# One encoder step on a TensorE-bound core: remainders of ten weight tiles made by an adding DMA in place of eight native fp32 steps, and six sample products earlier

## The chip, the cores and the metric

The kernel runs on one core of a Trainium2 chip. TensorE (PE in the profile) multiplies; VectorE (DVE), ScalarE (ACT) and GpSimd (POOL) do the rest; transfers are issued from SyncE (SP) and from POOL. The metric is device time in microseconds of one execution: 2345.04 us before, the median of three runs from 2344.96 to 2345.13.

## The reference

A streaming encoder of two layers, for 256 prompt tokens and 8 x 16 sample tokens, 384 rows of 1024. Each layer is a mixer (a state-space one in layer 0, sliding-window attention in layer 1), and behind it a PEER layer, where the change lies. PEER is a mixture of 128 x 128 = 16384 experts of one row each:

```python
        cand = (v1[..., :, None] + v2[..., None, :]).reshape(PEER_TOKEN_BLOCK, PEER_HEADS, PEER_TOPK * PEER_TOPK)
        vs, ci = lax.top_k(cand, PEER_TOPK)
        eid = (e1 * PEER_NKEYS + e2).reshape(PEER_TOKEN_BLOCK, PEER_HEADS * PEER_TOPK)
        gate = jax.nn.softmax(vs.astype(jnp.float32), axis=-1).reshape(PEER_TOKEN_BLOCK, PEER_HEADS * PEER_TOPK)
        ue = jnp.take(u_tab, eid, axis=0)
        act = jax.nn.gelu(jnp.einsum('tkd,td->tk', ue, xb).astype(jnp.float32))
        ve = jnp.take(v_tab, eid, axis=0)
        return jnp.einsum('tk,tkd->td', (gate * act).astype(xb.dtype), ve)
```

Each token has a query for each of 8 heads; the best 16 of 128 first keys and of 128 second keys give 256 sums, the best 16 of which name the experts. So every token takes 128 rows of `u`, weighs gelu of its products with them by a softmax, and adds that many rows of `v`. All is float32.

## The kernel before

A PEER layer of this kernel has three stages. The **query phase** multiplies all 384 rows by the query weights in 16 tiles. **u** multiplies the prompt's 256 tokens with *all* 16384 rows of `u`, 128 rows a step, in 128 steps; each step leaves a 128 x 256 block in a big array `G` (two halves, `G[0]` and `G[1]`, 64 steps each). **V** multiplies `G`, once it is weighed by the gates, with all rows of `v`, again in 128 steps. The sample's 128 tokens don't use the dense products: POOL gathers each token's rows of `u` (128 gathers, one for each place k, into a ring of three tiles `gath`), and DVE multiplies and sums each with the tokens (`u_item`, a *sample product*). `tick(s)` sets when: the table `U_DUE` says how many of the 128 products must have been recorded by step s (0 to 63 is u's first half, 64 to 127 its second, 128 on V).

A float32 product is *split* on PE: ACT rounds a weight tile to `hi` (line 129), DVE makes the remainder `lo` = raw - hi (line 130), and `gemm_cols` (lines 165 to 167) adds hi x hi, hi x lo and lo x hi, 24 matmuls a step in u, and 12 by two in V (line 180). A *native* step multiplies float32 tiles as they are, with an exact copy `xf` of the tokens in u (lines 1212 and 1567) and `G` itself in V (line 1642), 8 instructions each without a remainder. Before, `NATIVE` names eight of u's steps and `NATIVE_V` twelve of V's. `hi` and `lo` go round in rings of two, to which two more are lent in the first half's first 56 steps (`more`); `raw` has four.

Beside u's first half runs the *routing*: Python generators, of which each `pull` records a piece. `sample` routes the sample's tokens, then `prompt` the 256 prompt tokens in two blocks. A piece is a top-16 (lines 1268 to 1272), the decoding of places (`decode`, one-hot products at 1323 and 1327, folds at 1331, sums `ES` at 1334) or the end (`route_end`: softmax, transposes on PE at 1363, copies at 1366, and for the sample the indices `eidU` at 1380). `route_end` yields `DELAY` times before its transposes, and for the sample a second time before its indices. In the loop over the first half's steps each step pulls two pieces of `sample` until it ends; only from then on does it pull one or two pieces of `prompt` and call `tick`. What `prompt` still holds after step 63 is recorded behind the loop. The second half needs all of it: `w_prep` builds from it one-hot tiles (`ob`, `og`, `oa`), `w_apply` multiplies them on PE (line 1609), `w_mult` puts the result on `G` (line 1615).

The order on each engine: in the query phase and u's first half a tile scheduler orders instructions by its own clock; in u's second half and in V they stand on PE, DVE, ACT and POOL as written. Buffers and semaphores follow from the rings.

Of the kernel before, what the change touches and what calls it, by code (L numbers as in the profile page):

```python
# [9 lines left out]
F32 = mybir.dt.float32  # L10
F32R = mybir.dt.float32r
# [4 lines left out]
AF = mybir.ActivationFunctionType  # L16
OP = mybir.AluOpType
AX = mybir.AxisListType

P = 128  # L20
D = 1024
KD = D // P
NB = 3
NP = 256
# [20 lines left out]
RG = 32 // GR  # L45
TURN = 8
GSCALE = 2.0 ** 15
NATIVE = range(4, 56, 7)
NATIVE_V = range(3, 63, 5)
TAIL = 2  # L50
DONE = (2, 0, 1)
GLAG = 2
DELAY = (4, 8)
EARLY = (4, 1)

GD = 2
# [1 line left out]
I_DUE = (206, 250)  # L58
PACE = 1.5
AHEAD = 2 * 64 - 5  # L60
U_DUE = ((64, 22), (128, 68), (192, 115), (206, P))
V_DUE = [82, 85, 90, 96, 103, 148, 156, 162, 167, 173, 178, 183, 188, 193, 199, 211,
         217, 222, 227, 232, 237, 243, 247, 252]
V_SLOTS = [(1, e, 66, 64 + e) for e in range(28, 60, 4)] + [(0, e, 128 + e + 5, 256) for e in (0, 4, 8, 12, 20, 24, 28, 32, 56, 60)] + [(0, 16, 209, 256)]
# [3 lines left out]
def encoder_step(ctx: ExitStack, tc: tile.TileContext, t_in, t_out):  # L68
    nc = tc.nc
    sync, act, dve, pool, pe = nc.sync, nc.scalar, nc.vector, nc.gpsimd, nc.tensor  # L70
    n_names = [0]

    def T(pl, shape, dt=F32, tag=None, bufs=None):
        n_names[0] += 1
        return pl.tile(shape, dt, tag=tag, name=f"{tag}_{n_names[0]}", **({} if bufs is None else {"bufs": bufs}))
# [41 lines left out]
    gcol = T(const, [P, 5, KD], F32, tag="gcol")  # L117
# [29 lines left out]
    def load_raw(src, n=D):  # L147
        raw = ring(n, F32, "raw", 4)
        sync.dma_start(raw, src)
        return raw  # L150

    def load_split(src, n=D):
        return split_raw(load_raw(src, n), n)
# [63 lines left out]
    def fill(pl):  # L217
        T(pl, [P, 56], F32, tag="fill")
# [909 lines left out]
    def peer(l):  # L1128
        with ExitStack() as c:
# [13 lines left out]
            G = [T(gpools[0], [P, HE, NP], F32, tag="G0"), None]  # L1143
# [32 lines left out]
            turned = {}  # L1176
# [27 lines left out]
            close_h()  # L1204
            xfctx = tc.tile_pool(name="pxf", bufs=1, side="right")
            xfpool = xfctx.__enter__()
            xf = T(xfpool, [P, KD, NP], F32, tag="xf")
            fill(xfpool)

            def exact(k):  # L1210

                act.activation(xf[:, k], turned[k][:, :NP], AF.Copy, scale=gcol[:, 2 + l, k:k + 1])

            def ready(k):
                return split(qhi[:, k], qlo[:, k], turned[k], scale=gcol[:, 2 + l, k:k + 1])

            with in_order():
                turn(range(6), [2])
                ahead = [bank([P, NT]) for _ in range(2)]
                hi1 = ring(D, F32R, "hi", 2)  # L1220
                lo1 = ring(D, F32R, "lo", 2)
                act.copy(hi1, raws[1])
                for k in range(KD):
                    ready(k)
                    if k in (1, 2):
                        exact(k - 1)
                    ks = slice(k * P, (k + 1) * P)
                    pe.matmul(ahead[0], wq[0][0][:, ks], qhi[:, k], start=(k == 0), stop=False)
                    pe.matmul(ahead[1], hi1[:, ks], qhi[:, k], start=(k == 0), stop=False)
                    pe.matmul(ahead[0], wq[0][0][:, ks], qlo[:, k], start=False, stop=False)  # L1230
                    pe.matmul(ahead[1], hi1[:, ks], qlo[:, k], start=False, stop=False)
                    pe.matmul(ahead[0], wq[0][1][:, ks], qhi[:, k], start=False, stop=(k == KD - 1))
                    if k in (1, 2):
                        turn([k + 5], range(NB))
                for k in range(2, KD):
                    exact(k)
                dve.tensor_tensor(lo1, raws[1], hi1.bitcast(F32), op=OP.subtract)
                for k in range(KD):
                    pe.matmul(ahead[1], lo1[:, k * P:(k + 1) * P], qhi[:, k], start=False, stop=(k == KD - 1))
                wq.append(load_split(t_in["p_w_q"][l, 2]))  # L1240
# [100 lines left out]
            def route_end(b):  # L1341
# [10 lines left out]
                if b == 2:  # L1352
                    dve.tensor_scalar(es[0], es[0], float(NKEY), float(l * NKEY * NKEY), op0=OP.mult, op1=OP.add)
                    dve.tensor_tensor(es[0], es[0], es[1], op=OP.add)
                for _ in range(DELAY[b == 2]):
                    yield
# [10 lines left out]
                if b == 2:  # L1367
                    lay = T(one, [P, GR + 1, P], F32, tag="gath", bufs=3)
                    for g_ in range(GR + 1):
                        dve.tensor_tensor(lay[:, g_].rearrange("p (q c r) -> p q c r", c=4, r=RG),  # L1370
                                          (group(ps[:, 1], g_) if g_ < GR else group(ps[:, 0], GD)).unsqueeze(1).to_broadcast([P, GR, 4, RG]),
                                          same_q.unsqueeze(2).unsqueeze(3).to_broadcast([P, GR, 4, RG]), op=OP.mult)
                    for _ in range(DELAY[1]):
                        yield
# [40 lines left out]
            for ct in range(2 * PH):  # L1415
                if ct < 2:
                    ps = ahead[ct]
                else:
                    ps = bank([P, NT])
# [136 lines left out]

            def u_weights(e2):

                if e2 in NATIVE:
                    return load_raw(t_in["u_t"][l, e2]), None  # L1560
                return load_split(t_in["u_t"][l, e2])

            def u_products(e2, wt):
                ps = bank([P, NP])
                if wt[1] is None:
                    for k in range(KD):
                        pe.matmul(ps, wt[0][:, k * P:(k + 1) * P], xf[:, k], start=(k == 0), stop=(k == KD - 1))  # L1567
                else:
                    gemm_cols(ps, wt, xs[0], xs[1], 0, NP)
                return ps  # L1570

            def u_gelu(e2, ps):
                act.activation(G[e2 // HE][:, e2 % HE], ps, AF.Gelu_apprx_tanh)
# [46 lines left out]
            def v_weights(e2):  # L1620

                if e2 in NATIVE_V:
                    return load_raw(vtab[e2]), None
                return load_split(vtab[e2])

            def v_acts(e2):

                if e2 in NATIVE_V:
                    return None
# [29 lines left out]
            start = [0]  # L1659

            def tick(s):

                room[0] = min(room[0] + PACE, PACE)
                s0, n0 = start[0], 0
                for s1, n1 in U_DUE:
                    if s < s1:
                        break
                    s0, n0 = s1, n1
                want = P if s >= U_DUE[-1][0] else n0 + (n1 - n0) * (s + 1 - s0) // (s1 - s0)
                while done["u"] < want:  # L1670
# [29 lines left out]

            busy = True
            xs = [qhi, qlo]
            for e2 in range(HE):
                j = e2 - (HE - TURN)
                if j == 0:
                    more.clear()
                    lent.__exit__(None, None, None)
                    xfctx.__exit__(None, None, None)
                    xpool = tc.tile_pool(name="px", bufs=1, side="right")
                    xp = xpool.__enter__()  # L1710
                    xhi = T(xp, [P, KD, NP], F32R, tag="xhi")
                    xlo = T(xp, [P, KD, NP], F32R, tag="xlo")
                    T(xp, [P, 8], F32, tag="gap")
                u_gelu(e2, u_products(e2, u_weights(e2)))
                if j >= 0:
                    ks = slice(2 * (j // 2), 2 * (j // 2) + 2)
                    x_, q_ = ((xhi, qhi), (xlo, qlo))[j % 2]
                    pin(act.copy(x_[:, ks], q_[:, ks, :NP]))
                if busy:
                    busy = pull(sample, 2)  # L1720
                    if not busy:
                        start[0] = e2 + 1
                        fetch_u(0)
                        fetch_u(1)
                else:
                    pull(prompt, 2 if e2 % 4 == 0 else 1)
                    tick(e2)
# [17 lines left out]
            wt = u_weights(HE)  # L1745
            held = in_order(HELD + (mybir.EngineType.Pool,))
            held.__enter__()
            for e2 in range(HE):
# [8 lines left out]
                wt = nxt  # L1757
# [19 lines left out]
            for e2 in range(2 * HE):  # L1777
                if mult:
                    w_mult(*mult.pop())
                while n < 2 * HE and n <= e2 + (2 if n < AHEAD else 1):  # L1780
                    if n == AHEAD:
                        more.clear()
                    wt = v_weights(n)
# [154 lines left out]
```

## Time and profile before

| | |
|---|---|
| median of three runs | 2345.04 us |
| the profiled execution's own time, its span | 2350.95 us, 2349.2 us |
| PE busy in the span | 2295.5 us (98%) |
| DVE, ACT, POOL busy | 1982.0 (84%), 1252.2 (53%), 764.2 us (33%) |
| layer 0: u's first half, second half, V | 453 to 649, 649 to 866, 866 to 1265 us |
| layer 1: u's first half, second half, V | 1514 to 1713, 1713 to 1926, 1926 to 2330 us |
| DMA share in u's first half, in V | 0.57 to 0.71, 0.99 |

A row of the timeline is start, duration, engine, line, operation and tiles, with the idle time before it and what ended that in brackets. Durations overlap a little: an instruction of DVE starts some 0.08 us before the one ahead of it is through, so what one costs is read from start to start.

### The profile page before, as it was taken

What the parts mean: (1) busy time and instruction counts of PE and PEld (TensorE: products, weight loads), DVE (VectorE), ACT (ScalarE), POOL (GpSimd) and SP (SyncE); (2) the same over time, 40 slices, a digit from 0 to 9 for tenths busy, and PEclk for the clock granted to TensorE, in tenths of its full rate; (3) what the DMA queues carried; (4) which work ended last, traced back from release to release, by engine and by line L of the source; (5) the groups of instructions that cost most, each with busy time, mean ns of one, the idle gap of its engine ahead of it and who ended that gap; (6) DMA issues with size and microseconds to landing.
All of it is one profiled execution on the core that took longest, in us unless ns stands there. A gap on an engine that the chain in (4) does not pass through costs nothing. (4 is left out here: it accounts for less than half of the span.)

```text
span 2349.2 us, 43880 instructions
## 1 busy us (share of the span) xinstructions
PE 2295.5 (98%) x16340; PEld 1957.4 (83%) x16341; DVE 1982.0 (84%) x4235; ACT 1252.2 (53%) x2393; POOL 764.2 (33%) x779
## 2 busy tenths in 40 slices
PE   7999999999999999999999999999999999999998
PEld 6899988999998997667776778999999997667775
DVE  5999956979988999888876676979998999888876
ACT  5665624344466676554444555334476666554443
POOL 1323300012245334545563100011145324545562
PEclk9999999999999999999999999999999999999999
DMA  5554444366799889999996515367799889999997
GB/s 200 188 194 174 160 152 162 130 220 243 252 349 340 302 309 325 385 370 398 409 419 259 164 64 179 120 208 250 238 355 339 315 306 331 384 367 394 413 419 280
DMA packets 178086, 649.72 MB, mean 277 GB/s; under 512 B 21248, under 2 KB 23152, under 8 KB 175472
## 3 DMA queue, kind: packets, MB, share of 16 engines
q1 hardware_dynamic: 100944, 365.85, 42.6%
q0 software_dynamic: 76928, 281.07, 32.0%
q8 instruction: 128, 2.10, 0.4%
q14 instruction: 86, 0.70, 0.1%
HBM read 630.62 MB, written 18.06 MB: 276 GB/s over the span
## 5 line engine op out<-in xcount | busy, mean ns | idle before, releaser
L129 ACT CAST hi<-raw 128x1024 fp32r<-128x1024 f32 (+1 forms) x426 | 444.2, 1043 | 607.1 <-PE bank L166 251.6
L130 DVE TENSOR_TENSOR lo<-raw,hi 128x1024 fp32r<-128x1024 f32 (+1 forms) x426 | 515.4, 1210 | 172.8 <-ACT hi L129 151.8
L1434 POOL DMA_INDIRECT gath<-in_p_u,eidU x226 | 292.2, 1293 | 830.6 <-DVE gath L1483 514.0
L167 PE MATMUL bank<-xhi,lo 128*128 128x256 f32 (+1 forms) x1088 | 307.4, 282 | 6.1 <-DVE lo L130 3.8
L165 PE MATMUL bank<-xhi,hi 128*128 128x256 f32 (+1 forms) x1088 | 311.6, 287 | 0.0
L166 PE MATMUL bank<-xlo,hi 128*128 128x256 f32 (+1 forms) x1088 | 305.3, 281 | 0.0
L1434 POOL DMA_INDIRECT G<-in_p_v,eidT x192 | 222.8, 1160 | 76.4 <-issue 53.6
L165 PE MATMUL bank<-qhi,hi 128*128 128x256 f32 (+1 forms) x784 | 232.3, 296 | 0.0
L167 PE MATMUL bank<-qhi,lo 128*128 128x256 f32 (+1 forms) x784 | 227.0, 290 | 2.2 <-DVE lo L130 2.2
L166 PE MATMUL bank<-qlo,hi 128*128 128x256 f32 (+1 forms) x784 | 228.1, 291 | 0.0
L167 PEld LDWEIGHTS bank<-xhi,lo 128*128 128x128 f32 x1088 | 204.4, 188 | 10.2 <-DVE lo L130 7.2
L1597 ACT ACTIVATE oa<-ioh,e2T 128x128 f16<-128x128 f16 x512 | 163.3, 390 | 92.2 <-PE bank L1609 71.4
L165 PEld LDWEIGHTS bank<-xhi,hi 128*128 128x128 f32 x1088 | 204.5, 188 | 9.5 <-issue 5.7
L180 PE MATMUL bank<-hi,phi 128*128 128x512 f32 x632 | 206.1, 405 | 1.5 <-ACT phi L129 1.5
L129 ACT CAST hix<-raw 128x1024 fp32r<-128x1024 f32 x118 | 123.9, 1050 | 156.7 <-PE bank L180 56.8
L166 PEld LDWEIGHTS bank<-xlo,hi 128*128 128x128 f32 x1088 | 204.5, 188 | 0.6 <-issue 0.2
L180 PE MATMUL bank<-lo,phi 128*128 128x512 f32 x632 | 197.7, 392 | 0.9 <-DVE lo L130 0.9
L180 PE MATMUL bank<-hi,plo 128*128 128x512 f32 x632 | 196.4, 390 | 0.0
L130 DVE TENSOR_TENSOR lox<-raw,hix 128x1024 fp32r<-128x1024 f32 x118 | 143.6, 1217 | 19.6 <-ACT hix L129 15.2
L180 PEld LDWEIGHTS bank<-hi,phi 128*128 128x128 f32 x632 | 113.6, 188 | 49.4 <-ACT phi L129 19.1
L167 PEld LDWEIGHTS bank<-qhi,lo 128*128 128x128 f32 x784 | 147.7, 188 | 2.6 <-DVE lo L130 2.6
L166 PEld LDWEIGHTS bank<-qlo,hi 128*128 128x128 f32 x784 | 148.5, 189 | 0.4
(416 smaller groups left out, 5518.5 us busy)
## 6 DMA issues: line engine op xcount, KB each, us to landing
raw<-in_u_t SPq DMA_DIRECT2D x256, 512.0 KB
raw<-in_p_v SPq DMA_DIRECT2D x256, 512.0 KB
raw<-in_w_in SPq DMA_DIRECT2D x32, 512.0 KB
raw<-in_p_w_q SPq DMA_DIRECT2D x32, 512.0 KB
raw<-in_w_z SPq DMA_DIRECT2D x16, 512.0 KB
s<-in_state_ssm SPq DMA_DIRECT2D x8, 1024.0 KB
out_sm_ssm<-s SPq DMA_DIRECT2D x8, 1024.0 KB
raw<-in_w_out SPq DMA_DIRECT2D x16, 512.0 KB
```

Of the source, the lines that this page charges most:

```text
L129: act.copy(hi, raw)
L130: dve.tensor_tensor(lo, raw, hi32, op=OP.subtract)
L165: pe.matmul(ps, whi[:, s], xhi[:, k, c0:c1], start=(k == 0), stop=False)
L166: pe.matmul(ps, whi[:, s], xlo[:, k, c0:c1], start=False, stop=False)
L167: pe.matmul(ps, wlo[:, s], xhi[:, k, c0:c1], start=False, stop=(k == KD - 1))
L180: mm = pe.matmul(halves[hf], x, w[:, hf * n:(hf + 1) * n], start=s_, stop=e_)
L1434: pool.indirect_dma_start(out=tile_, out_offset=None, in_=tab, in_offset=bass.IndirectOffsetOnAxis(ap=idx, axis=0))
L1597: act.activation(a[:, i], ioh, AF.Square, scale=-1.0, bias=e2T[:, t, 0:1])
```

## The change

In u's first half the eight native steps go. Instead, for the ten steps of `BY_DMA` (4, 9, ... 49), `u_ahead` loads the raw tile by SP into a place of `G[0]` that is written late (52 to 56 or 56 to 60, in turn); `u_summed` has ACT write `dhi`, the rounded tile, and `dlo`, the negated raw tile, and has POOL issue a DMA that adds the raw tile to `dlo`. The products of such a step are the same 24 matmuls, with the 16 on `dhi` first and the 8 on `dlo` last. It is called four steps ahead of its use; `dhi` and `dlo` have one tile each, where `xf` stood. In V, nine steps are native instead of twelve. `DELAY`'s second number, for the sample, goes from 8 to 12. `U_DUE` asks for 28 sample products by step 64 instead of 22, 72 by step 128 instead of 68, and as many as before from there on.

```diff
--- before.py
+++ after.py
@@ -45,12 +45,13 @@
 RG = 32 // GR
 TURN = 8
 GSCALE = 2.0 ** 15
-NATIVE = range(4, 56, 7)
-NATIVE_V = range(3, 63, 5)
+BY_DMA = range(4, 53, 5)
+BY_DMA_AHEAD = 4
+NATIVE_V = range(4, 63, 7)
 TAIL = 2
 DONE = (2, 0, 1)
 GLAG = 2
-DELAY = (4, 8)
+DELAY = (4, 12)
 EARLY = (4, 1)
 
 GD = 2
@@ -58,7 +59,7 @@
 I_DUE = (206, 250)
 PACE = 1.5
 AHEAD = 2 * 64 - 5
-U_DUE = ((64, 22), (128, 68), (192, 115), (206, P))
+U_DUE = ((48, 15), (64, 28), (128, 72), (192, 115), (206, P))
 V_DUE = [82, 85, 90, 96, 103, 148, 156, 162, 167, 173, 178, 183, 188, 193, 199, 211,
          217, 222, 227, 232, 237, 243, 247, 252]
 V_SLOTS = [(1, e, 66, 64 + e) for e in range(28, 60, 4)] + [(0, e, 128 + e + 5, 256) for e in (0, 4, 8, 12, 20, 24, 28, 32, 56, 60)] + [(0, 16, 209, 256)]
@@ -1204,13 +1205,7 @@
             close_h()
             xfctx = tc.tile_pool(name="pxf", bufs=1, side="right")
             xfpool = xfctx.__enter__()
-            xf = T(xfpool, [P, KD, NP], F32, tag="xf")
-            fill(xfpool)
-
-            def exact(k):
-
-                act.activation(xf[:, k], turned[k][:, :NP], AF.Copy, scale=gcol[:, 2 + l, k:k + 1])
-
+            summed = {}
             def ready(k):
                 return split(qhi[:, k], qlo[:, k], turned[k], scale=gcol[:, 2 + l, k:k + 1])
 
@@ -1222,8 +1217,6 @@
                 act.copy(hi1, raws[1])
                 for k in range(KD):
                     ready(k)
-                    if k in (1, 2):
-                        exact(k - 1)
                     ks = slice(k * P, (k + 1) * P)
                     pe.matmul(ahead[0], wq[0][0][:, ks], qhi[:, k], start=(k == 0), stop=False)
                     pe.matmul(ahead[1], hi1[:, ks], qhi[:, k], start=(k == 0), stop=False)
@@ -1232,8 +1225,6 @@
                     pe.matmul(ahead[0], wq[0][1][:, ks], qhi[:, k], start=False, stop=(k == KD - 1))
                     if k in (1, 2):
                         turn([k + 5], range(NB))
-                for k in range(2, KD):
-                    exact(k)
                 dve.tensor_tensor(lo1, raws[1], hi1.bitcast(F32), op=OP.subtract)
                 for k in range(KD):
                     pe.matmul(ahead[1], lo1[:, k * P:(k + 1) * P], qhi[:, k], start=False, stop=(k == KD - 1))
@@ -1556,15 +1547,37 @@
 
             def u_weights(e2):
 
-                if e2 in NATIVE:
-                    return load_raw(t_in["u_t"][l, e2]), None
-                return load_split(t_in["u_t"][l, e2])
+                return summed.pop(e2, None) or load_split(t_in["u_t"][l, e2])
+
+            raws_ = {}
+
+            def u_ahead(e2):
+
+                e = 52 + 4 * (BY_DMA.index(e2) % 2)
+                raws_[e2] = G[0][:, e:e + 4].rearrange("p e t -> p (e t)")
+                sync.dma_start(raws_[e2], t_in["u_t"][l, e2])
+
+            def u_summed(e2):
+
+                raw = raws_.pop(e2)
+                hi = T(xfpool, [P, D], F32R, tag="dhi")
+                lo = T(xfpool, [P, D], F32R, tag="dlo")
+                if e2 == BY_DMA[0]:
+                    fill(xfpool)
+                act.copy(hi, raw)
+                act.activation(lo, raw, AF.Copy, scale=-1.0)
+                pool.dma_start(lo.bitcast(F32), raw, accum_op=OP.add)
+                summed[e2] = hi, lo
 
             def u_products(e2, wt):
                 ps = bank([P, NP])
-                if wt[1] is None:
+                if e2 in BY_DMA:
+                    for x in xs:
+                        for k in range(KD):
+                            pe.matmul(ps, wt[0][:, k * P:(k + 1) * P], x[:, k, :NP],
+                                      start=(x is xs[0] and k == 0), stop=False)
                     for k in range(KD):
-                        pe.matmul(ps, wt[0][:, k * P:(k + 1) * P], xf[:, k], start=(k == 0), stop=(k == KD - 1))
+                        pe.matmul(ps, wt[1][:, k * P:(k + 1) * P], xs[0][:, k, :NP], start=False, stop=(k == KD - 1))
                 else:
                     gemm_cols(ps, wt, xs[0], xs[1], 0, NP)
                 return ps
@@ -1700,6 +1713,7 @@
 
             busy = True
             xs = [qhi, qlo]
+            u_ahead(BY_DMA[0])
             for e2 in range(HE):
                 j = e2 - (HE - TURN)
                 if j == 0:
@@ -1712,6 +1726,10 @@
                     xlo = T(xp, [P, KD, NP], F32R, tag="xlo")
                     T(xp, [P, 8], F32, tag="gap")
                 u_gelu(e2, u_products(e2, u_weights(e2)))
+                if e2 + BY_DMA_AHEAD in BY_DMA:
+                    u_summed(e2 + BY_DMA_AHEAD)
+                    if e2 + BY_DMA_AHEAD + 5 in BY_DMA:
+                        u_ahead(e2 + BY_DMA_AHEAD + 5)
                 if j >= 0:
                     ks = slice(2 * (j // 2), 2 * (j // 2) + 2)
                     x_, q_ = ((xhi, qhi), (xlo, qlo))[j % 2]
```

Lines below are those of the program they belong to; the changed one's are some 8 lower. The first place is DVE at the end of u's first half in layer 0. Before, from the second one-hot product of the last prompt piece on, through the remainders of steps 59, 60 and 61, to the first copies of the transposed sums:

```order
L1327 TENSOR_TENSOR oh_6882<-oh_6882,ixb_6880 128x2048
L130 TENSOR_TENSOR lo_7010<-raw_7007,hi_7009 128x1024
L1483 SCALAR_TENSOR_TENSOR gath_6845,au_5239<-gath_6845,xg_3874 128x1024
L1331 TENSOR_TENSOR oh_6882<-oh_6882 128x8x128
L130 TENSOR_TENSOR lo_7046<-raw_7043,hi_7045 128x1024
L1331 TENSOR_TENSOR oh_6882<-oh_6882 128x8x64
L1331 TENSOR_TENSOR oh_6882<-oh_6882 128x8x32
L1334 TENSOR_TENSOR ES_5927<-oh_6882 128x64 x2
L1483 SCALAR_TENSOR_TENSOR gath_6774,au_5239<-gath_6774,xg_3874 128x1024
L130 TENSOR_TENSOR lo_7087<-raw_7084,hi_7086 128x1024
L1366 COPY gcols_7076<-bank_7077 128x128
L1366 CAST e1T_3683<-bank_7077 128x256
```

And in the changed kernel, from the remainder of step 65 (`lo_7382`) on; the remainder of step 66 comes behind the copies that follow here:

```order
L131 TENSOR_TENSOR lo_7382<-raw_7379,hi_7381 128x1024
L1595 TENSOR_TENSOR ob_7410<-ioh_74,e1T_3683 128x512
L1314 TENSOR_TENSOR oh_7188<-ij_7150,io_637_3870 128x2048
L1474 SCALAR_TENSOR_TENSOR gath_7057,au_5405<-gath_7057,xg_3864 128x1024
L1598 TENSOR_TENSOR og_7412<-ob_7410,g_601_3685 128x1024
L1613 TENSOR_TENSOR oa_7420<-ioh_74,e2T_3684 128x512
L1318 TENSOR_TENSOR oh_7188<-oh_7188,ixb_7186 128x2048
L1474 SCALAR_TENSOR_TENSOR gath_7232,au_5405<-gath_7232,xg_3864 128x1024
L1322 TENSOR_TENSOR oh_7188<-oh_7188 128x8x128
L1474 SCALAR_TENSOR_TENSOR gath_7275,au_5405<-gath_7275,xg_3864 128x1024
L1322 TENSOR_TENSOR oh_7188<-oh_7188 128x8x64
L1322 TENSOR_TENSOR oh_7188<-oh_7188 128x8x32
L1325 TENSOR_TENSOR ES_6156<-oh_7188 128x64 x2
```

The one-hot products, folds and sums of the last prompt piece, which stood between the remainders of steps 58 to 61, now stand behind that of step 65, with the gate tiles of the second half and four sample products among them. The second place is PE, where step 60's last matmul and the transposes of the gates and sums into one bank stood before so:

```order
L167 MATMUL bank_7049<-qhi_3702,lo_7046 128x256
L1363 MATMUL bank_7077<-ident_69,gate_6967 128x128
L1363 MATMUL bank_7077<-ident_69,ES_5927 128x128
L165 MATMUL bank_7090<-qhi_3702,hi_7086 128x256
L1363 MATMUL bank_7077<-ident_69,ES_5927 128x128
L166 MATMUL bank_7090<-qlo_3703,hi_7086 128x256
L167 MATMUL bank_7090<-qhi_3702,lo_7087 128x256
L165 MATMUL bank_7090<-qhi_3702,hi_7086 128x256
```

And now, from the last matmuls of step 63, on `qhi` and `qlo`, to the first of step 64, on `xhi` and `xlo`:

```order
L167 MATMUL bank_7320<-qlo_3703,hi_7316 128x256
L168 MATMUL bank_7320<-qhi_3702,lo_7317 128x256
L1354 MATMUL bank_7351<-ident_69,gate_7268 128x128
L1354 MATMUL bank_7351<-ident_69,ES_6156 128x128 x2
L166 MATMUL bank_7385<-xhi_7005,hi_7375 128x256
L167 MATMUL bank_7385<-xlo_7006,hi_7375 128x256
L168 MATMUL bank_7385<-xhi_7005,lo_7376 128x256
```

The three transposes went from beside step 61 to the place between steps 63 and 64.

## The prediction

> **What bounds the kernel now.** I read the busy line of the page first, then the busy time by stretches of layer 0.
>
> ```profile
> PE 2295.5 (98%) x16340; PEld 1957.4 (83%) x16341; DVE 1982.0 (84%) x4235; ACT 1252.2 (53%) x2393; POOL 764.2 (33%) x779
> ...
> 452.80:505.00 52.20, 51.55 (x419) 50.52 (x418) 40.81 (x144) 24.04 (x36) 4.65 (x4) 1.00 0.57 192
> 505.00:580.00 75.00, 75.00 (x599) 73.34 (x598) 70.02 (x255) 32.14 (x49) 14.64 (x10) 1.00 0.70 245
> 580.00:649.00 69.00, 67.96 (x563) 66.93 (x563) 67.46 (x224) 34.32 (x54) 13.67 (x11) 1.00 0.71 249
> 649.00:700.00 51.00, 48.43 (x495) 46.71 (x495) 45.35 (x69) 36.72 (x78) 26.50 (x23) 1.00 0.95 358
> 700.00:866.00 166.00, 164.56 (x1671) 154.30 (x1670) 150.28 (x230) 110.56 (x225) 63.35 (x53) 1.00 0.88 315
> 920.00:1265.00 345.00, 345.00 (x1896) 247.75 (x1895) 287.93 (x433) 169.23 (x303) 185.64 (x153) 1.00 0.99 391
> ```
>
> The columns after the stretch are its length, then PE, weight loads, DVE, ACT and POOL busy, the granted clock, the DMA share and GB/s. TensorE sets the pace: in u's first half (452.8 to 649) it is busy 194.5 of 196.2 us, from 700 to 866 164.6 of 166, in V all of 345. But in the first half VectorE is nearly as full: from 505 to 649 it is idle 144 - 70.02 - 67.46 = 6.5 us. So an edit that lightens PE there can only gain if DVE comes along. ACT has half of its time free, and the DMA share of 0.57 to 0.71 stands against 0.99 in V.
>
> **The change on PE.** Each layer loses eight native products in u and three in V; the steps become split products of 24 and 12 matmuls.
>
> ```profile
> 464.38 3.61 PE L1567 MATMUL bank<-xf,raw 128*128 128x256 f32 x16
> 467.64 0.47 PE L165 MATMUL bank<-qhi,hi 128*128 128x256 f32 x1
> ...
> 470.56 0.28 PE L165 MATMUL bank<-qhi,hix 128*128 128x256 f32 x1
> ...
> 473.29 0.27 PE L1363 MATMUL bank<-ident,gate 128*128 128x128 f32 x1
> ```
> ```profile
> 883.91 0.70 PE L180 MATMUL bank<-hi,phi 128*128 128x512 f32 x2
> ...
> 886.76 3.59 PE L1642 MATMUL bank<-raw,G 128*128 128x512 f32 x8
> 890.19 0.63 PE L1609 MATMUL bank<-og,oa 128*128 128x64 f16 x16
> ```
>
> A native step and the split step behind it go from 464.38 to 470.56, 6.18 us; the next split step goes from 470.56 to 473.29, 2.73. So a native step is 3.45. A split step is 2.73 here, and at most (196.2 - 8 x 3.45) / 56 = 3.0 with all other matmuls of the stretch counted in; I take 2.80, near the lower end, since few other matmuls lie between, and 0.65 us saved for each: 8 x 0.65 = 5.2 us a layer. In V the native step is 890.19 - 886.76 = 3.43, the split one 886.76 - 883.91 = 2.85, 0.6 to 0.75 saved with its spread over other steps; 3 x 0.7 = 2.1 us a layer. Those three steps need three more remainders on DVE, while four sample products of the same length leave that stretch, so DVE is not worse there. PE alone would give -2 x (5.2 + 2.1) = -14.6 us.
>
> **The change on DVE.** Two remainders fewer in the first half (54 of 64 steps instead of 56), and six sample products more (28 instead of 22). And the order moves: the prompt's pieces are pulled only once the sample's are through, which `DELAY` puts eight pulls, four steps, later, so the end of the prompt's routing is recorded behind the loop. In the order its last part, with the sums `ES`, stands on DVE behind the remainder of step 65, and on PE its three transposes, which stood beside step 61, stand between steps 63 and 64. PE cannot begin step 64 before them. What that piece takes is read from the same instructions before:
>
> ```profile
> 631.98 1.22 DVE L1327 TENSOR_TENSOR oh<-oh,ixb 128x2048 bf16<-128x2048 bf16 x1
> 633.12 1.22 DVE L130 TENSOR_TENSOR lo<-raw,hi 128x1024 fp32r<-128x1024 f32 x1
> ...
> 635.39 0.69 DVE L1331 TENSOR_TENSOR oh<-oh 128x1024 bf16<-128x1024 bf16 x1
> 636.00 1.22 DVE L130 TENSOR_TENSOR lo<-raw,hi 128x1024 fp32r<-128x1024 f32 x1
> 637.13 0.74 DVE L1331 TENSOR_TENSOR oh<-oh 128x512 bf16<-128x512 bf16 x2
> 637.91 0.36 DVE L1334 TENSOR_TENSOR ES<-oh 128x64 f32<-128x64 bf16 x2
> 638.19 1.22 DVE L1483 SCALAR_TENSOR_TENSOR gath<-gath,xg 128x1024 f32<-128x1024 f32 x1
> 639.33 0.08 DVE L1483 DVE_READ_ACCUMULATOR gath<-gath,xg 128x1 f32 x1
> ...
> 647.16 1.23 DVE L130 TENSOR_TENSOR lo<-raw,hi 128x1024 fp32r<-128x1024 f32 x1
> 649.88 1.23 DVE L130 TENSOR_TENSOR lo<-raw,hi 128x1024 fp32r<-128x1024 f32 x1 [1.50 <-ACT hi L129]
> 651.03 0.41 DVE L1582 TENSOR_TENSOR ob<-ioh,e1T 128x512 f16<-128x512 f16 x1
> 651.48 0.69 DVE L1585 TENSOR_TENSOR og<-ob,g 128x1024 f16<-128x1024 f16 x1
> 652.09 0.42 DVE L1600 TENSOR_TENSOR oa<-ioh,e2T 128x512 f16<-128x512 f16 x1
> ```
>
> A row's start to the next row's start is what it holds DVE for: 1.15 us for a remainder, 1.14 for `oh<-oh,ixb` (the other one-hot product has the same shape) and for a sample product; 0.61 for the first fold of `oh`, 0.7 for the other two, 0.28 for `ES`, 0.45 for `ob`, 0.61 for `og`, 0.4 for `oa`. From the start of step 65's remainder to the end of `ES` the changed order has one remainder, `ob`, `og`, `oa`, two one-hot products, three folds, two sums and three sample products: 1.15 + 0.45 + 0.61 + 0.4 + 2 x 1.14 + 0.61 + 0.7 + 0.28 + 3 x 1.14 = 9.9 us. With 0.4 for the three transposes (the one at 473.29 above is busy 0.27, and such matmuls overlap), step 64 starts 10.3 us after the remainder of step 65.
>
> When does that remainder start? Before, the rows of step 63's last and step 64's first product, and of ACT's cast for step 65, are these:
>
> ```profile
> 648.60 0.28 PE L167 MATMUL bank<-qhi,lo 128*128 128x256 f32 x1
> 648.71 0.28 PE L165 MATMUL bank<-xhi,hi 128*128 128x256 f32 x1
> ...
> 648.79 1.05 ACT L129 CAST hi<-raw 128x1024 fp32r<-128x1024 f32 x1 [0.88 <-PE bank L166]
> ```
>
> The cast of step 65 waited for step 63's last use of the buffer, and its remainder followed at 649.88, 1.17 us after PE was through with step 63. This ring is as short after the change. If PE sets the pace, step 63 ends at 648.71 - 5.2 = 643.5, the remainder of step 65 starts at 644.7, and step 64 at 655.0: an idle PE for 11.5 us, and 6.3 us later than before. If DVE sets the pace: up to step 65's remainder it has two remainders fewer and two sample products more (24 of the 28), and 5.2 us of routing less (2 x 1.14 + 0.61 + 0.7 + 0.28, and 1.3 behind the transposes). Against that stands the later start of the samples: its indices come four steps later.
>
> ```profile
> 492.57 0.29 DVE L1380 CAST eidU<-bank 128x128 int32<-128x128 f32 x1 [3.75 <-PE bank L1378]
> 493.14 1.06 POOL L1434 DMA_INDIRECT gath<-in_p_u,eidU  x1 [97.39 <-DVE gU L1381]
> 498.56 1.22 DVE L1483 SCALAR_TENSOR_TENSOR gath<-gath,xg 128x1024 f32<-128x1024 f32 x1 [5.61 <-DMA gath<-in_p_u,eidU]
> ```
>
> Here DVE has nothing to do for 3.75 and 5.61 us, and four steps more of waiting (11.2 us) are filled with remainders and pieces of routing to about half, 6 us lost. That makes step 65's remainder 0.8 us later than 647.16 + 1.14 = 648.3, 649.1, and step 64 start at 659.4: 10.7 later than before. Of the 6.5 us that DVE had idle a part takes this up. Between 6.3 and 10.7 I take **7.7 us a layer**, nearer to the lower end, since PE is the fuller of the two.
>
> **What follows behind the stall.** In the second half the DVE waits of PE may be given back, since loads and casts run ahead while PE stands still.
>
> ```profile
> PE bank L167 <- DVE lo L130: 2.4, 4, 0.9
> PE bank L167 <- issue: 1.4, 2, 0.9
> PE bank L167 <- DVE lo L130: 1.2, 2, 0.8
> PE bank L167 <- issue: 0.4, 1, 0.4
> ```
>
> These are all waits of PE in u's second half (total, times, longest), the first two rows of layer 0, the last two of layer 1: 3.8 and 1.6 us, 2.7 on average. More than that cannot come back there, and nothing may. I take all of it, for two sample products (2.3 us of DVE) leave this stretch too.
>
> **The adding DMA.** Its chain for one step is a cast, a gelu and a negated copy on ACT (at most three times the 1.05 us of a cast, 3.2), the issue on POOL, and the landing; its low products need it 4 steps and 16 of 24 matmuls after the buffers come free, 4 x 2.8 + 1.9 = 13.1 us. With 1.1 for the issue the landing has 8.8 us. No such transfer is in this trace; the nearest row is the gather issued at 493.14, whose product starts at 498.56, 5.4 us later. At two steps (29 and 49) the adding DMA stands on POOL's queue behind a gather that waits for a sample product, which comes after the remainder of three steps earlier: 3 x 2.8 + 1.9 - 1.14 - 1.3 - 1.1 = 6.8 us are left. Between 5.4 and an unknown upper end I take 5.4: hidden, no cost. The rows of POOL's issues beside a busy DVE:
>
> ```profile
> 565.50 0.94 POOL L1434 DMA_INDIRECT gath<-in_p_u,eidU  x1 [16.20 <-DVE gath L1483]
> ...
> 586.92 1.88 POOL L1434 DMA_INDIRECT gath<-in_p_u,eidU  x1 [6.76 <-DVE t L1306]
> ```
>
> An issue takes between 0.94 and 1.88 us. [...]
>
> ACT gets 18 casts more in the first half (54 + 10 + 10 instead of 56), 19 us of its 106 free. The ten raw copies are loads that were there before, on SP's queue, into other tiles; each waits there for the adding DMA of ten steps earlier, and the queue runs several steps ahead. In the query phase eight exact copies of 0.47 us leave ACT, and the first `dhi` and `dlo` come in, 2.1 us:
>
> ```profile
> 379.71 0.47 ACT L1212 ACTIVATE xf<-bank,gcol 128x256 f32<-128x256 f32 x1 [1.85 <-DMA hd<-h]
> ```
>
> Between a wait of 1.85 us gone and 2.1 us on the path I take nothing.
>
> **Sum.** A layer: 7.7 - 2.7 - 2.1 = +2.9 us; two layers +5.8. The profiled execution took 2350.95 us (span 2349.2), 5.9 over the median of the three runs, 2345.04; on the median the sum gives **2350.8**. Low end of the case: 6.3 - 3.8 - 2.1 = 0.4 in one layer, 6.3 - 1.6 - 2.1 = 2.6 in the other, 2348, and 2344 with both query waits gone; high end: 10.7 a layer with nothing given back, 2366.
>
> **Rivals.**
> - *No stall.* DVE reaches the routing's end early enough, and the whole gain on PE stays: 2345.0 - 14.6 = 2330.4. The 98% of PE speak for it; the order of PE and DVE, fixed with the transposes between steps 63 and 64, speaks against it.
> - *The stall is paid back.* If u's second half or V, freed of six products, gave back 5.6 us a layer instead of 2.7, the time would be 2345. Against it: from 700 to 866 PE has only 1.4 us idle.
> - *The adding DMA comes late*, on the other side and worse. It decides from 8.8 us of landing (6.8 at two steps). A landing of 10 us would cost 8 x 1.2 + 2 x 3.2 = 16 us a layer, 2350.8 + 32 = 2383. For it speaks that it reads its destination too and shares 16 engines with loads; against it the gathers' 5.4 us.
>
> **Numbers.** Forecast case 0.64, no stall 0.10, paid back 0.16, late adding DMA 0.10. The range 2342 to 2366 leaves out the first and the last rival; the likeliest case's own range is 2344 to 2366. About 0.2%, 4.7 us, is what can be told from no change: below 2340.3 is the first rival and a little of the third case's spread, 0.15; within it most of the paid-back case and the lower part of the forecast's, 0.29; slower 0.56.
>
> **What would show it.** PE idle for 9 to 14 us in front of the first product of step 64, in both layers, put down to the sums or to a one-hot product on DVE; step 63 ending 2 to 5 us earlier than before. Low products of the adding steps without a wait; if their wait is more than 1 us the third rival is at work. I am wrong if PE passes from step 63 to 64 in under 3 us, or if the second half or V is shorter by over 6 us a layer.

## The result: slower by 0.8%, and the profile after

The changed kernel takes 2365.05 us (median of four runs, 2363.03 to 2365.86) against 2345.0 for the kernel before: ratio 1.0077, 95% interval 1.0064 to 1.0091. The prediction was 2350.8, with 2342 to 2366 as its range: the sign was right, the loss of 20 us more than three times the 5.8 of its sum. The profiled execution took 2365.83 us (span 2364.0), 14.9 more than that of before.

First the waits of PE, in u of layer 0 and of layer 1 (total, times, longest):

```profile
PE bank L1354 <- DVE ES L1325: 14.0, 1, 14.0
PE bank L168 <- DVE lo L131: 2.2, 5, 0.6
...
PE bank L1354 <- DVE ES L1325: 13.5, 1, 13.5
PE bank L168 <- DVE lo L131: 2.7, 6, 0.6
```

The one large wait of each layer is that of the transposes for the sums `ES`, between steps 63 and 64. There is none on `dlo`. DVE in the stretch ahead of them (L131, L1325, L1354 and L1474 are what L130, L1334, L1363 and L1483 were before):

```profile
645.20 1.23 DVE L1474 SCALAR_TENSOR_TENSOR gath<-gath,xg 128x1024 f32<-128x1024 f32 x1 [2.33 <-DMA gath<-in_p_u,eidU]
...
646.75 1.22 DVE L131 TENSOR_TENSOR lo<-raw,hi 128x1024 fp32r<-128x1024 f32 x1
...
655.18 1.23 DVE L1474 SCALAR_TENSOR_TENSOR gath<-gath,xg 128x1024 f32<-128x1024 f32 x1 [0.78 <-DMA gath<-in_p_u,eidU]
...
657.12 0.36 DVE L1325 TENSOR_TENSOR ES<-oh 128x64 f32<-128x64 bf16 x2
...
663.08 1.23 DVE L131 TENSOR_TENSOR lo<-raw,hi 128x1024 fp32r<-128x1024 f32 x1 [2.74 <-ACT hi L130]
```

Step 65's remainder starts at 646.75, `ES` is done at 657.4: 10.7 us against the 9.9 of the sum, the rest being 0.78 us for a gather. Three sample products stand between the two, as the prediction counted; the fourth comes only behind `ES`. The remainder itself came late, behind a sample product that waited 2.33 us for its row (1.61 and 0.91 us are the same two waits in layer 1). Then the windows around the stall, with PE's granted clock behind the five busy times, and PE's rows after it:

```profile
643.00:657.50 14.50, 0.47 (x5) 0.24 (x3) 11.42 (x22) 4.01 (x9) 4.05 (x4) 0.63 0.64 214
657.50:660.00 2.50, 2.50 (x12) 2.50 (x13) 2.46 (x7) 0.00 (x0) 0.13 (x1) 0.50 0.71 202
660.00:664.00 4.00, 4.00 (x34) 4.00 (x33) 1.23 (x3) 1.33 (x2) 2.72 (x5) 0.93 0.46 149
664.00:668.00 4.00, 4.00 (x48) 3.96 (x46) 3.22 (x7) 2.72 (x6) 2.78 (x3) 1.00 0.73 242
```
```profile
657.40 0.69 PE L1354 MATMUL bank<-ident,ES 128*128 128x128 f32 x2 [14.03 <-DVE ES L1325]
...
658.74 0.41 PE L167 MATMUL bank<-xlo,hi 128*128 128x256 f32 x1
658.95 0.41 PE L168 MATMUL bank<-xhi,lo 128*128 128x256 f32 x1
...
661.44 0.28 PE L168 MATMUL bank<-xhi,lo 128*128 128x256 f32 x1
```

PE comes out of the idle time at half clock (granted 0.50 from 657.5 to 660.5): a matmul every 0.21 us instead of 0.12, for some 3 us, which costs about 1.5 us. In layer 1, behind 13.5 us of idleness, the granted clock was 0.50 from 1728.5 to 1732. The prediction had not counted it. How short an idle time has such a stretch behind it, these rows do not show.

The account, by the gelu of a step on ACT (its start, before and after) and by V's first and last product on PE:

| | before | after | moved by | forecast |
|---|---|---|---|---|
| layer 0, step 0 | 458.1 | 456.9 | -1.2 | 0 |
| layer 0, step 63 | 650.1 | 644.6 | -4.3 | -5.2 |
| layer 0, step 64 | 653.3 | 662.9 | +15.1 | +12.9 |
| layer 0, step 127 | 861.7 | 866.9 | -4.4 | -2.7 |
| layer 0, V | 420.3 long | 418.1 long | -2.2 | -2.1 |
| to layer 1, step 0 | 1519.0 | 1524.5 | +2.5 | 0 |
| layer 1, step 63 | 1713.0 | 1715.8 | -2.7 | -5.2 |
| layer 1, step 64 | 1716.3 | 1734.1 | +15.0 | +12.9 |
| layer 1, step 127 | 1921.0 | 1938.0 | -0.8 | -2.7 |
| layer 1, V | 420.3 long | 418.1 long | -2.2 | -2.1 |

The column "moved by" adds up to the 14.8 us by which the spans differ; it counts each row from the one above it. Of the 2.5 us up to layer 1's step 0, some 1.6 lie in that layer's mixer, where the granted clock was 0.83 over 10 us (1379 to 1389; before 1.00 in the same place). The other 5 of the 20 are in the reference point: the profiled execution of before was 5.9 us over its own median, that of after 0.8 over its. Executions of one kernel differ with the mean granted clock (the kernel before took 2338.59 us at 0.999 and 2350.11 at 0.994 on one chip), so a single one can lie some 6 us off the median.

### The profile page after: what moved, and what is told of

Read it like the earlier page. It is cut to its first block, busy times and chain, and to the rows that moved or that the text cites. A ratio compares the mean times of both kernels' runs of the same rounds, so it can differ in the third digit from the quotient of the medians.

```text
span 2364.0 us, 44273 instructions
## 1 busy us (share of the span) xinstructions
PE 2287.3 (97%) x16492; PEld 1964.0 (83%) x16493; DVE 1987.3 (84%) x4243; ACT 1287.6 (54%) x2425; POOL 794.4 (34%) x799
## 5 line engine op out<-in xcount | busy, mean ns | idle before, releaser
L130 ACT CAST hi<-raw 128x1024 fp32r<-128x1024 f32 (+1 forms) x428 | 446.2, 1043 | 608.7 <-PE bank L167 307.8
L131 DVE TENSOR_TENSOR lo<-raw,hi 128x1024 fp32r<-128x1024 f32 (+1 forms) x428 | 518.1, 1211 | 163.7 <-ACT hi L130 161.5
L1425 POOL DMA_INDIRECT gath<-in_p_u,eidU x228 | 298.0, 1307 | 581.3 <-DVE gath L1474 431.6
L166 PE MATMUL bank<-qhi,hi 128*128 128x256 f32 (+1 forms) x768 | 225.9, 294 | 0.0
L130 ACT CAST hix<-raw 128x1024 fp32r<-128x1024 f32 x118 | 124.2, 1053 | 176.9 <-PE bank L181 101.0
L181 PE MATMUL bank<-hi,plo 128*128 128x512 f32 x648 | 201.3, 390 | 0.0
L131 DVE TENSOR_TENSOR lox<-raw,hix 128x1024 fp32r<-128x1024 f32 x118 | 143.8, 1218 | 29.0 <-ACT hix L130 28.9
L1474 DVE SCALAR_TENSOR_TENSOR gath<-gath,xg 128x1024 f32<-128x1024 f32 x116 | 141.0, 1215 | 17.5 <-DMA gath<-in_p_u,eidU 17.5
```

Source lines behind the costliest of these rows:

```text
L130: act.copy(hi, raw)
L131: dve.tensor_tensor(lo, raw, hi32, op=OP.subtract)
L166: pe.matmul(ps, whi[:, s], xhi[:, k, c0:c1], start=(k == 0), stop=False)
L181: mm = pe.matmul(halves[hf], x, w[:, hf * n:(hf + 1) * n], start=s_, stop=e_)
L1425: pool.indirect_dma_start(out=tile_, out_offset=None, in_=tab, in_offset=bass.IndirectOffsetOnAxis(ap=idx, axis=0))
L1474: pin(dve.scalar_tensor_tensor(tile_, tile_, 1.0, xg[g], op0=OP.mult, op1=OP.mult, accum_out=au[g][:, j:j + 1]))
```

## The experiments

Ratios are to the kernel before on the same chip, with 95% intervals.

| run | median us | before, us | ratio | interval |
|---|---|---|---|---|
| DELAY back to 8 | 2359.23 | 2347.44 | 1.0037 | 1.0022 to 1.0051 |
| more prompt pulls | 2383.34 | 2347.44 | 1.0143 | 1.0120 to 1.0166 |
| old product table | 2357.46 | 2347.44 | 1.0046 | 1.0031 to 1.0061 |
| before, DELAY 12 alone | 2365.39 | 2347.44 | 1.0072 | 1.0050 to 1.0094 |
| DMA and V alone | 2339.22 | 2347.10 | 0.9969 | 0.9953 to 0.9985 |
| before, new table alone | 2366.77 | 2347.10 | 1.0094 | 1.0073 to 1.0115 |
| DMA and V, filled | 2337.70 | 2347.10 | 0.9970 | 0.9953 to 0.9987 |
| before, filled | 2345.93 | 2347.10 | 0.9995 | 0.9981 to 1.0010 |
| before, new table, no gathers | 2353.51 | 2343.69 | 1.0040 | 1.0027 to 1.0054 |
| changed, no gathers | 2360.85 | 2343.69 | 1.0078 | 1.0062 to 1.0095 |
| before, no gathers | 2344.47 | 2343.69 | 1.0002 | 0.9989 to 1.0014 |
| DMA's remainders by DVE | 2356.46 | 2343.69 | 1.0052 | 1.0036 to 1.0069 |

### The tail moved forward, in two ways

The prediction's theory was that the *place* of the routing's tail (the one-hot products, sums and transposes of its last piece) costs the time. Two kernels move it back, with all the rest as changed.

```diff
-DELAY = (4, 12)
+DELAY = (4, 8)
```

> The changed kernel with DELAY back at (4, 8), all else as changed; the sums of the last prompt piece then stand on DVE behind the remainder of step 63 instead of 65. Theory (the routing's tail behind step 65 is the whole loss): the idle PE of 14.0 and 13.5 us before step 64 and the 2 us of half clock behind it go, some 2.6 us a layer of what the second half gave back go with them: 2365 - 2 x (14 + 2 - 2.6) = 2338 us, under 2345. Rival (the adding DMA and its traffic on POOL, SP and the DMA engines cost the time): over 2355, with PE waiting on dlo or on hi. Second rival (DVE is full with 28 products, whatever the order): the stall goes elsewhere in the first half, 2345 to 2350.

```diff
-                    pull(prompt, 2 if e2 % 4 == 0 else 1)
+                    pull(prompt, 2 if e2 % 2 == 0 else 1)
```

> The changed kernel with two prompt pieces pulled in every second step instead of every fourth, DELAY still (4, 12), so that the routing ends beside step 60 as before the change. Tail theory: as with DELAY 8 or a little better, since all of the routing ends three steps before step 64: 2330 to 2338 us, no idle PE over 2 us between steps 63 and 64. Rival (the adding DMA costs): over 2355. Rival (DVE full): 2345 to 2350, with the waits on lo of the first half grown to 5 us or more a layer.

Measured 2359.23 and 2383.34: that the place is the whole loss falls. The first kernel gets about half of it back (1.0037 against 1.0077), the second loses more. In the first the sums stand ahead of step 64's remainder and the 14 us are gone, but the waits of PE on remainders grew (the waits of PE, u of layer 0), the longest of them where DVE itself had waited for a gather's row (DVE's timeline):

```profile
PE bank L168 <- DVE lo L131: 7.4, 6, 2.4
```
```profile
640.56 1.23 DVE L1474 SCALAR_TENSOR_TENSOR gath<-gath,xg 128x1024 f32<-128x1024 f32 x1 [3.46 <-DMA gath<-in_p_u,eidU]
```

In the second PE stood for 4.35 us in front of the gates' transpose, which was recorded earlier than DVE had the gates, and for remainders after that (the waits of its u in layer 0, then two rows of PE):

```profile
PE bank L168 <- DVE lo L131: 10.8, 12, 3.5
PE bank L1354 <- DVE gate L1341: 4.3, 1, 4.3
```
```profile
629.36 0.33 PE L1354 MATMUL bank<-ident,gate 128*128 128x128 f32 x1 [4.35 <-DVE gate L1341]
...
641.78 0.58 PE L168 MATMUL bank<-qhi,lo 128*128 128x256 f32 x1 [3.49 <-DVE lo L131]
```

So with the tail pulled forward PE waits for DVE at other places. Neither kernel waits for `dlo` by more than 0.3 us, though both times lie where the expectation put the adding DMA's rival; that rival had to be tried by itself.

### Each part alone

With the old table and the new DELAY:

```diff
-U_DUE = ((48, 15), (64, 28), (128, 72), (192, 115), (206, P))
+U_DUE = ((64, 22), (128, 68), (192, 115), (206, P))
```

> The changed kernel with the old table of sample products (22 by step 64, 68 by step 128), DELAY still (4, 12). The tail stands behind step 65's remainder as in the change. Tail theory: the stall stays, shorter by three products of 1.14 us and by the 2.3 and 0.8 us for which DVE waited for gathers: 7 to 8 us idle, 2365 - 2 x 6.5 = 2352 us. Rival (the six extra products are the cause): no stall, 2340 or less.

Then the kernel before with the new DELAY alone, and with the new table alone:

```diff
-DELAY = (4, 8)
+DELAY = (4, 12)
```

> The kernel before with DELAY (4, 12) alone: native steps, no adding DMA, 22 products. Tail theory: the routing's tail falls behind step 65 here too; idle PE of 7 to 8 us before step 64, 1.5 to 2 us of half clock, 2.6 us given back: +6.5 a layer, 2358 us. Rival (the loss needs the adding DMA or the extra products): within 3 us of 2345.

```diff
-U_DUE = ((64, 22), (128, 68), (192, 115), (206, P))
+U_DUE = ((48, 15), (64, 28), (128, 72), (192, 115), (206, P))
```

> The kernel before with the new table of sample products alone (28 by step 64, 72 by step 128), native steps and DELAY (4, 8) kept. VectorE-bound theory: six products more are 6.9 us of DVE, of which the 6.5 us idle from 505 to 649 can take a part; 2 to 4 us a layer lost at step 64, 1 to 2 of it given back: 2347 to 2352 us. Rival (the products cost nothing, since PE is the bound): 2343 to 2346.

The old table leaves 7.2 us of the stall, as expected, and the loss falls to 1.0046, some 10 us (2352 us, 7 more than before, were expected). And before with DELAY alone loses about as much as the whole change (1.0072; 13 us were expected, 18 measured), with this wait in each layer:

```profile
PE bank L1363 <- DVE ES L1334: 6.9, 1, 6.9
```

DELAY gives DVE no work. What it does is leave DVE without work early. These are the windows from 500 to 520 us of before, then of before with DELAY 12; the third busy time is DVE's:

```profile
500.00:520.00 20.00, 20.00 (x161) 19.59 (x160) 17.75 (x65) 7.41 (x13) 3.73 (x3) 1.00 0.70 245
```
```profile
500.00:520.00 20.00, 20.00 (x148) 19.58 (x148) 8.54 (x23) 6.36 (x10) 4.63 (x4) 0.93 0.63 215
```

There DVE waits for the sample's indices and for its first row (5.0 and 5.1 us in the changed kernel, which has the same DELAY) while the prompt's pieces are not yet pulled. From 457 to 640 us it is busy 159.5 us instead of 166.1, 6.6 us less (4.4 in the same stretch of layer 1), against the stall of 6.9. That the stall comes from this idle time, and not from the order at the half's end, is argued from these sums; no run keeps DELAY 12 and fills the time.

And before with the new table alone comes to 1.0094, some 20 us where 2 to 7 were expected of 6.9 us of DVE work a layer. Its waits of PE in u of layer 0, and of DVE from 500 to 670:

```profile
PE bank L167 <- DVE lo L130: 9.6, 10, 3.3
```
```profile
DVE gath L1483 <- DMA gath<-in_p_u,eidU: 6.6, 4, 2.4
```

Then both back in the changed kernel, which leaves the adding DMA and V's steps:

```diff
-DELAY = (4, 12)
+DELAY = (4, 8)
-U_DUE = ((48, 15), (64, 28), (128, 72), (192, 115), (206, P))
+U_DUE = ((64, 22), (128, 68), (192, 115), (206, P))
```

> The changed kernel with DELAY (4, 8) and the old table of sample products: what is left of the change are the ten adding DMAs in place of eight native steps, and nine native steps in V instead of twelve. Theory now (VectorE is the bound of the first half: every us that it idles early, or gets more to do, comes out at its end, as waits on lo or as the stall, wherever the order puts it): DVE has two remainders fewer, so PE's gain stays for the most part: step 64 starts 3 to 5 us earlier in each layer, V is 2.2 us shorter, 2345 - 2 x (3.5 + 2.2) = 2334 us. Rival (the adding DMA costs in itself, by its traffic or its queues): 2345 or more, with PE, ACT or SP waiting on dlo.

2339.22 us, 0.9969: faster than before (the interval ends at 0.9985) though short of the 2334 expected, step 64's gelu in layer 0 at 648.5 instead of 653.3, no stall, and 3.3 us of waits for remainders in u:

```profile
PE bank L168 <- DVE lo L131: 3.3, 7, 0.8
```

So the adding DMA is not what cost the time. Put together, with each part on or off (V's steps have no run of their own):

| | DELAY 8 | DELAY 12 |
|---|---|---|
| before, old table | 1 | 1.0072 |
| before, new table | 1.0094 | not run |
| DMA and V, old table | 0.9969 | 1.0046 |
| DMA and V, new table | 1.0037 | 1.0077 |

In both kernels the later sample alone costs 17 to 18 us and the earlier products alone 16 to 22; the two together, in the kernel with the DMA, 25, less than their sum. The issue and landing of the adding DMA, in the changed kernel:

```profile
L1569 POOL DMA_DIRECT2D dlo<-G x20: 855/971/992, 383.2 to 1658.2; - x20
...
DMA to landing us min/median/max: 4.8/6.6/11.0
```

The median of 6.6 us is within the 8.8 (6.8 at two steps) that the prediction allowed. The slowest is not: issued at 557.5, it landed 11.0 us later, 1.3 us before the product that needs it (569.8), so that nothing waited. What the adding DMA is worth shows when, in the kernel with the DMA and V alone, DVE makes the same ten remainders a layer (the lines show what the edit comes to):

```diff
-                act.copy(hi, raw)
-                act.activation(lo, raw, AF.Copy, scale=-1.0)
-                pool.dma_start(lo.bitcast(F32), raw, accum_op=OP.add)
-                summed[e2] = hi, lo
+                summed[e2] = split(hi, lo, raw)
```

> The changed kernel with DELAY (4, 8), the old table, and the ten remainders subtracted by DVE where the adding DMA made them (that one with the DMA: 2339.2 us). DVE gets 10 x 1.15 = 11.5 us more in each layer's first half and ACT 10.5 less. DVE-bound theory: 3 to 8 us a layer lost, 2345 to 2356 us. Rival (DVE has room, and the gain came from the native steps' absence alone): 2336 to 2342.

1.0052 against 0.9969: 20 remainders of 1.15 us, 23 us of DVE, cost about 19 us of the kernel's time, at the upper end of what was expected. In layer 0 the loss shows at two places: PE's granted clock is 0.83 from 480 to 500 us (with the DMA 1.00), and in the second half PE waits 5.6 us for remainders (with the DMA 2.6). It does not follow that DVE sets the pace of the first half in the kernel with the DMA and V alone. There PE waits for remainders only this long in layer 0 up to step 64 (452 to 648 us; 0.8 in layer 1), and the rest of the 3.3 us lies in the second half:

```profile
PE bank L168 <- DVE lo L131: 0.7, 2, 0.4
```

### Filling DVE's idle time

In the kernel with the DMA and V alone, and in the kernel before:

```diff
                     busy = pull(sample, 2)
+                    if e2 >= 6:
+                        pull(prompt, 1)
```

> As the last but one (adding DMA, DELAY (4, 8), old table), and one prompt piece pulled in each step from step 6 on while the sample's routing still goes on, so that DVE has work in the time that it waits for the sample's indices (three such waits, 3 to 6 us each). VectorE-bound theory: 2 to 4 us a layer less than without the filling: about 2328 us, with the waits on lo at the end of the first half gone. Rival (only the order at the half's end counts): the same as without.

> The kernel before with the same filling alone. PE is the bound there with 194 of 196 us busy, so the filling has nothing to give in the first half: 2343 to 2346 us by both theories; if it gains over 4 us, DVE was the bound of the kernel before too.

Nothing in either: 0.9970 beside 0.9969, and 0.9995. The first was expected to gain 2 to 4 us a layer and missed; its profile shows DVE waiting for ACT's casts instead, 7.0 us in ten waits (500 to 670, layer 0):

```profile
DVE lo L131 <- ACT hi L130: 7.0, 10, 1.5
```

And ACT's casts wait for PE to be through with a buffer (44.8 us in 31 waits there). The window of PE, weight loads and DVE in the filled kernel shows why no time came of it:

```profile
520.00:640.00 120.00, 120.00 (x1041) 120.00 (x1041) 112.64 (x356) 66.55 (x99) 32.64 (x24) 1.00 0.84 275
```

PE is busy without a gap; its waits for remainders up to step 64, 0.7 and 0.8 us without the filling, are gone, and little more was there to be had. The expectation looked for the waits at the end of the first half, but most of the 3.3 us lies behind it.

### Without the gathers' latency

Products 16 to 39 use what the three `gath` tiles hold; DVE has as many instructions as before, though the scheduler may order them otherwise. This is done in before with the new table, in the changed kernel, and in before as it was (two more lines, which keep the tiles in `kept`, are not shown).

```diff
+                    if 16 <= k < 40:
+                        urows[k] = kept[k % 3]
+                        return
```

> The kernel before with the new table of sample products (as two runs ago, 2366.8 us), and without the gathers of products 16 to 39: these multiply what lies in the three tiles already, so DVE has the same instructions and no gather to wait for at the half's end. Left out: those gathers, and with them the right values of the sample products 16 to 39. Theory (products that stand close together wait for their gathers, three tiles with 7 to 8 us from one product to the row of the third next one, and remainders wait behind them in DVE's order): most of the 20 us go, 2347 to 2354. Rival (DVE's own work is too much): 2360 or more, the waits of PE on lo as before (9.6 and 8.2 us).

> The changed kernel without the gathers of products 16 to 39 (left out as in the last one). Gather theory: DVE's waits of 2.3 and 0.8 us in the piece ahead of step 64's transposes go, the stall of 14 us becomes 11, as the sum of DVE's instructions alone gives it; behind it the products of the second half have no wait either: 2365 - 2 x 3 to 5 = 2355 to 2359 us. Rival (work alone): 2363 or more.

> The kernel before without the gathers of products 16 to 39, nothing else: the control for the two others. There the products stand apart, and DVE waits for no gather from product 2 on but once: 2342 to 2347 us by the gather theory. If POOL's issues or the DMA traffic of the gathers slowed the loads, it would gain as much as the other two.

The control is at 1.0002, so those gathers as such cost nothing where the products stand apart. Before with the new table falls from 1.0094 to 1.0040: DVE waits for no row from 500 to 670 any more, and PE for remainders 4.6 us instead of 9.6 in layer 0. So about half of what the earlier products cost is the time from a tile's release to its next row. In the changed kernel the stall shrinks:

```profile
PE bank L1354 <- DVE ES L1325: 9.8, 1, 9.8
...
PE bank L1354 <- DVE ES L1325: 9.9, 1, 9.9
```

Of the 4.2 and 3.6 us that went, 3.1 and 2.5 are DVE's waits for rows in that piece (2.33 and 0.78, in layer 1 1.61 and 0.91); the other 1.1 is one sample product, which stands behind `ES` here. The time stays at 1.0078, where 6 to 10 us less were expected: the profiled execution, 2357.54, is the fastest of its four, and the slowest is 2365.08. Shown is that the gathers made some 3 us of each stall; that they cost the changed kernel time is not.

## Why the prediction was right, and where it was not

**PE.** Near: 4.3 us saved from step 0 to step 63 in layer 0 (5.2 forecast), 2.2 in V (2.1). Layer 0's step 63 was 5.5 us earlier, but 1.2 of that came ahead of step 0, where the prediction had put nothing. In layer 1 only 2.7 came. The granted clock there was 0.92 from 1560 to 1566 and 0.79 from 1566 to 1580 (before: 0.89 from 1550 to 1566), which is 0.5 + 2.9 - 1.8 = 1.6 us, the difference between the layers.

**The stall.** Right in its place: the transposes between steps 63 and 64, held up by `ES`. Mis-sized: "an idle PE for 11.5 us". Its 9.9 us of work hold: from step 65's remainder to the end of `ES` it is 10.7 us with 0.78 for a row. What was missing are the 2.3 and 0.8 us for rows of gathers, since the sum took each instruction's own time and nothing for what it waits on, and 1.5 us of half clock. Measured from step 0, step 64 is 10.8 us later in layer 0 and 12.3 in layer 1, against the 7.7 taken and the upper bound of 10.7.

**The second half.** 4.4 and 0.8 us came back, 5.2 in all for the two layers against 5.4 forecast. The sum is right partly by luck: PE's waits there fell from 3.8 and 1.6 us to 0.9 in each layer, which is 3.6 of the 5.2, and where the rest lies is not settled.

**The adding DMA.** Right: hidden, no wait on it. Its landing was put at 5.4 us and took 6.6.

**Reading of the cause.** Half right. "And the order moves ... so the end of the prompt's routing is recorded behind the loop" was taken as the cause, and DELAY alone does cost 17 to 18 us, with the stall in that place. What the traces add is the DVE time that it leaves unused early; the prediction had priced this ("6 us lost"; 6.6 and 4.4 less busy in before with DELAY 12) but counted it only in its upper bound. Wrong is that nothing else was named, with "no stall" as what the other order would give, 2330.4: the six products alone cost as much. The prediction had the row for that too (6.5 us of DVE's idle time against 6.9 us of products, not counting their waits for rows), and used it only for the upper bound of step 65's remainder.

**The sum.** It was put on the median of before, 2345.04, with rows from an execution of 2350.95. What made that one 5.9 us slower was not in the changed kernel's, and that is 5 of the missing 14 us; where it lay is not settled. Step 64 in the two layers is 7.7 of them, the time ahead of the two steps 0 is 1.3.

**The range.** Its upper end, 2366, is 2345.04 + 2 x 10.7; it leaves out V's 2.1 us a layer, which the lower end counts. With them it is 2362.2, and the 2365.05 measured lies above. That the range held is luck.

## What to carry to other kernels

Before an engine's order alone is blamed for a wait, add up its work and its idle time in that stage. Here the engine behind the bound one, DVE, had only a few per cent idle (6.5 us of the 144 from 505 to 649), and work added to it cost time by itself (1.0094), as did a later start of work that it then did not have early (1.0072); moving the piece that is waited for recovered only half (1.0037 instead of 1.0077). Work moved into such a stage can cost more than its instructions: in the kernel before it was some 20 us for 13.8 us of products, where DVE also waited 6.6 us for rows in layer 0 and PE's granted clock was 0.92 and 0.91 in the two stretches of 10 us from 660 to 680. Of this change the adding DMA and the V steps are worth keeping (0.9969 together), the later sample and the earlier products are not.

## What the hardware showed

- An adding DMA of 512 KB within the core's memory landed 6.6 us after its issue (4.8 to 11.0), against 4.5 us (4.2 to 4.9) for a plain load of that size from outside in the same stretch. Of the queues only SP's waited for it (seven waits in layer 0, 51 us in all, while ACT waited for no load).
- After 14 us of idleness PE's matmuls came every 0.21 us for some 3 us, at a granted clock of 0.50, then every 0.12. The same pitch stood behind the 6.9 us of before with DELAY 12 (657.0 to 659.8; the granted clock was 0.64 from 657 to 661 and 1.00 from 661 to 665) and, in the kernel with more prompt pulls, behind 4.35 us (629.9 to 633.1) and behind 3.49 us (642.2 to 646.4).
- A sample product that needs a freed tile's next row can hold up DVE: in before with the new table DVE waited 6.6 us in four such waits, and for none once the gathers were left out.
